# A batched row gather: three direct batches in place of five, smaller first index group, ranks summed by TensorE, first slot table in PSUM

## Chip, cores, metric

One core of a Trainium2 chip. The metric is the device time of one execution in microseconds. For one core a run is called slow when it lies over 1.5% above the fastest of the same kernel on the same chip.

## The reference

```python
x: [32, 512, 1024] float32;  indices: [32, 128] int
for b in range(32):
    result[b] = x[b, indices[b]]        # 128 rows of 4 KB
```

The indices are drawn once, the same for every run. Of a batch's 128 indices 109 to 120 are distinct.

## The kernel before

Five "direct" batches are gathered by an indirect DMA straight into their output block and stored. The other 27 read each distinct row once: VectorE and TensorE work out which indices are first occurrences (`lead`), give each a slot (`rank`, `slot`, `pack`), and turn that into row numbers per slot (`at`; a slot without a row gets a number out of bounds, which the gather skips). The gather fills one of eight buffers `u`. TensorE then multiplies `u` with a 0/1 matrix `s` ("spread", four matmuls of 128x512), ScalarE copies the result to the output block, and SyncE issues the store. Index work goes in groups of three batches, four groups ahead. For the first such batch (`HALF`) rows 0 to 255 are loaded whole and early (1.05 MB), and `half_rows` spreads those.

```python
HEAD, RING, GROUP, AHEAD, FAR = 5, 8, 3, 4, 1024
HALF = HEAD
...
for b in range(HEAD):
    gather(blocks[b], first[...] if b == 0 else idxT[:, b:b + 1], b)
    store(b)
...
def step0(g):      # compare all pairs of indices of each batch of the group
    bcs[g] = bc = pbc.tile([N, 4, N], F32, name="bc")
    for k, b in enumerate(of_group(g)):
        pe(mm, bc[:, k], lhsT=ident[:, b:b + 1].to_broadcast([N, N]), rhs=vf[:], start=True, stop=True)
    for k, b in enumerate(of_group(g)):
        dve(v.scalar_tensor_tensor, out=junk[:], in0=bc[:, k], scalar=idxF[:, b:b + 1], in1=below[:], ..., accum_out=cnt[:, b:b + 1])
    ...
    dve(v.tensor_scalar, out=cols(lead, g), in0=cols(cnt, g), scalar1=0.0, scalar2=None, op0=ALU.is_equal)
    for b in of_group(g):
        if b < B - 2:
            dve(v.tensor_tensor, out=past[:, b + 1:b + 2], in0=past[:, b:b + 1], in1=lead[:, b:b + 1], op=ALU.add)

def step1(g):      # ranks -> slots -> pack
    pe(mm, rk[:], lhsT=above[:], rhs=cols(lead, g), start=True, stop=False)
    pe(mm, rk[:], lhsT=every[:], rhs=cols(past, g), start=False, stop=True)
    ...
def step2(g):      # row numbers `at`, matrices `s`
    ...
step0(0)
step0(1)
for g in range(AHEAD):
    step1(g)
    if 0 < g < AHEAD - 1:
        step0(g + 1)
    step2(g)
    for b in of_group(g):
        if b < HEAD + RING:
            fetch(b)
    if g == 0:
        half_spread()
    elif g < 3:
        half_rows(g - 1, False)
for b in range(HEAD, B):
    spread_rows(b)
    fetch(b + RING)                      # waits until TensorE is done with this u
    g, step = divmod(b - HEAD, GROUP)
    if g + AHEAD < GROUPS:
        (step0, step1, step2)[step](g + AHEAD)
```

## Time and profile before

| | before |
|---|---|
| median of all runs (lowest to highest) | 87.55 us (87.08 to 88.76) |
| span of the profiled run | 85.6 us |
| DMA: bytes, mean rate | 32.91 MB, 384 GB/s |
| busy: TensorE, VectorE, ScalarE, GpSimd | 72, 37, 47, 39% |
| u gathers: issue to landing, median | 15.2 us |

A gather lands 15 us after its issue, because it stands in a long queue (the very first gather, with no other ahead of it, landed after 5.2 us). The DMA is the bound, and the queue is its stock. The lines that carry this are in the prediction.

How to read the profile lines: PE is TensorE, DVE is VectorE, ACT is ScalarE, POOL is GpSimd, SPq is the queue of SyncE. A timeline line gives start, duration, engine, source line, operation and tiles; in brackets stands how long the engine had been idle before, and what ended that. A line by stretch gives the busy time of each engine and ends with the granted TensorE clock, the busy share of the DMA engines and the rate in GB/s.

### The profile page before, as it was taken

How to read it: one execution, taken by the hardware profiler on the slowest of the kernel's cores; microseconds unless marked ns; L12 is line 12 of the kernel's file. 1: busy time of each engine (PE TensorE's matmuls, PEld its weight loads, DVE VectorE, ACT ScalarE, POOL GpSimd, SP SyncE). 2: the span in 40 equal slices, each digit the busy share in tenths (PEclk: the TensorE clock that was granted, in tenths of full speed). 3: DMA queues.
4: the chain of work that ended last, by engine and by line, in shares of the span. 5: the costliest groups of instructions: out<-in, count | busy, mean ns of one | idle time of the engine just before them, and what ended most of it. 6: DMA issues, size and time to landing. Idle time of an engine off the chain costs nothing.

```text
span 85.6 us, 827 instructions
## 1 busy us (share of the span) xinstructions
PE 61.3 (72%) x189; PEld 25.3 (29%) x189; DVE 31.6 (37%) x160; ACT 40.5 (47%) x63; POOL 33.3 (39%) x43
## 2 busy tenths in 40 slices
PE   0320379576999999999878987878789888889300
PEld 0300242323434444444333433322223333323000
DVE  4498793786563864844641453000000000000000
ACT  0899930000665665555554354455544554446400
POOL 6587578727444455554332444443320000000000
PEclk9999999999999999999999999999999999999996
DMA  0799999999999999999999999999999999999980
GB/s 1 274 375 344 302 342 415 415 417 417 419 419 419 417 421 419 415 419 417 419 419 419 417 419 413 421 413 423 417 417 419 419 419 419 423 415 417 423 337 15
DMA packets 9636, 32.91 MB, mean 384 GB/s; under 512 B 1584, under 2 KB 1616, under 8 KB 9632
## 3 DMA queue, kind: packets, MB, share of 16 engines
q1 hardware_dynamic: 4736, 16.81, 48.2%
q0 software_dynamic: 4608, 15.01, 44.7%
q10 hardware_dynamic: 288, 1.05, 3.3%
q8 instruction: 1, 0.02, 0.1%
q14 instruction: 3, 0.02, 0.1%
HBM read 17.86 MB, written 16.78 MB: 404 GB/s over the span
## 4 chain that ended last, share of the span: by engine, by line
DMA 40%; PE 21%; issue 14%; DVE 14%; POOL 3%; ACT 1%; SPq 0%; POOLq 0%; DVEq 0%
DMA u<-in_x_dram,at 37%; PE ps L24 20%; DVE junk L24 3%; POOL u L121 3%; DVE pack L24 3%; DMA vals<-in_indices_dram 2%; DVE past L24 2%; DVE nth L24 2%; DVE s L24 1%; PE pos L24 1%; DVE slot L24 1%; ACT block L250 1%; DVE lead L24 1%; DVE same L24 1%; SPq L68 0%
## 5 line engine op out<-in xcount | busy, mean ns | idle before, releaser
L24 PE MATMUL ps<-u,s 128*128 128x512 f32 x108 | 52.4, 611 | 6.8 <-DMA u<-in_x_dram,at 6.2
L121 POOL DMA_INDIRECT u<-in_x_dram,at x27 | 26.9, 997 | 26.7 <-PE ps L24 5.8
L250 ACT COPY block<-ps 128x512 f32<-128x512 f32 x36 | 21.1, 585 | 18.7 <-PE ps L24 17.6
L24 PEld LDWEIGHTS ps<-u,s 128*128 128x128 f32 x108 | 18.3, 189 | 29.1 <-ACT block L250 14.8
L250 ACT COPY pair<-ps 128x512 f32<-128x512 f32 x16 | 9.4, 585 | 8.7 <-PE ps L24 7.1
L24 DVE SCALAR_TENSOR_TENSOR junk<-bc,idxF,below 128x128 f16<-128x128 f32 x27 | 8.0, 347 | 7.1 <-PE bc L24 7.1
L24 ACT COPY u<-zero 128x1024 f32<-128x1024 f32 x8 | 7.7, 1040 | 0.0
L24 PE MATMUL pos<-near,pack 128*128 128x1 f16 x27 | 2.0, 167 | 5.6 <-DVE pack L24 5.6
L240 ACT COPY block<-ps 128x512 f32<-128x512 f32 x2 | 1.2, 585 | 10.1 <-PE ps L24 10.1
L24 PE MATMUL ps<-early,same 128*128 128x512 f32 x8 | 5.7, 854 | 0.0
L24 DVE TENSOR_TENSOR pack<-turn,slot 128x384 f16<-128x384 f16 (+2 forms) x10 | 5.1, 518 | 0.3
L24 DVE TENSOR_TENSOR s<-bc,at 128x384 f32<-128x384 f32 x9 | 5.0, 558 | 0.3
L24 PEld LDWEIGHTS <-pack 128*128 128x128 f16 x27 | 1.7, 99 | 9.5 <-DVE pack L24 7.4
L24 DVE TENSOR_TENSOR past<-past,lead 128x1 f16<-128x1 f16 x25 | 4.1, 163 | 0.9
L24 PE MATMUL bc<-vf,ident 128*128 128x128 f16 x27 | 3.4, 256 | 1.3 <-DVE same L24 1.3
L121 POOL DMA_INDIRECT block<-in_x_dram,idxT x4 | 3.8, 947 | 1.3 <-issue 0.9
L24 PEld LDWEIGHTS <-ident 128*128 128x128 f16 x27 | 2.4, 111 | 4.2 <-issue 4.2
L24 DVE TENSOR_SCALAR at<-pos 128x3 int32<-128x3 f32 x9 | 1.4, 160 | 5.1 <-PE pos L24 4.8
L24 DVE CAST nth<-rk 128x3 int32<-128x3 f32 x9 | 1.4, 160 | 3.7 <-PE rk L24 3.3
L21 PE MATMUL pos<-ident,vf 128*128 128x32 f16 x1 | 0.2, 210 | 3.6 <-DVE vf L24 3.6
L24 ACT ACT_TABLE_LOAD x1 | 1.3, 1283 | 2.5 <-DVE vf L24 2.5
L24 PEld LDWEIGHTS ps<-early,same 128*128 128x128 f32 x8 | 1.9, 257 | 1.5 <-issue 1.5
(32 smaller groups left out, 18.4 us busy)
## 6 DMA issues: line engine op xcount, KB each, us to landing
out_dram<-block SPq DMA_DIRECT2D x24, 512.0 KB, 8.0
out_dram<-pair SPq DMA_DIRECT2D x4, 1024.0 KB, 11.1
early<-in_x_dram ACTq DMA_DIRECT2D x2, 512.0 KB, 3.8
u<-in_x_dram,at POOLq DMA_INDIRECT x27, 15.2
block<-in_x_dram,idxT POOLq DMA_INDIRECT x4, 6.4
vals<-in_indices_dram SPq DMA_DIRECT2D x1, 32.0 KB, 2.0
first<-in_indices_dram SPq DMA_DIRECT2D x1, 1.0 KB, 1.8
block<-in_x_dram,first POOLq DMA_INDIRECT x1, 5.2
```

Of the source, the lines that this page charges most:

```text
L21: self.last = do(*args, **kw)
L24: self.last = do(*args, **kw)
L121: nc.gpsimd.indirect_dma_start(out=dst, out_offset=None, in_=xf[:], in_offset=bass.IndirectOffsetOnAxis(ap=at, axis=0), element_offset=b * ...
L240: nc.scalar.copy(out=blocks[HALF][:, w], in_=ps[:])
L250: nc.scalar.copy(out=blocks[b][:, w], in_=ps[:])
```

## The change

The intent: a direct batch reads all its 128 rows, repeated ones too, so fewer direct batches are fewer bytes. For that the row numbers of the first other batch must be ready sooner, so the first group has two batches, and its work is shortened. The sums over earlier batches of the group go to TensorE (more matmuls into `rk`) and `past` is advanced once per group later on. The table that `pack` compares with lies in PSUM for the first group; the last two batches, in place of the last one, use the second table, which is laid out anew. The order of steps changes with it, and so does the place of `half_rows`. Cut to its core:

```diff
-    HEAD, RING, GROUP, AHEAD, FAR = 5, 8, 3, 4, 1024
+    HEAD, RING, GROUP, AHEAD, FAR = 3, 8, 3, 4, 1024
+    APART = B - 2
+    groups = [range(HEAD, HEAD + 2), *(range(b, b + GROUP) for b in range(HEAD + 2, B, GROUP))]
...
-        pe(mm, rk[:], lhsT=above[:], rhs=cols(lead, g), start=True, stop=False)
-        pe(mm, rk[:], lhsT=every[:], rhs=cols(past, g), start=False, stop=True)
+        earlier = [(k, lead[:, groups[g][0]:groups[g][0] + like - k]) for k in range(1, like)]
+        if g:
+            earlier.append((0, past[:, g:g + 1].to_broadcast([N, like])))
+        pe(mm, rk[:, :n], lhsT=above[:], rhs=cols(lead, g), start=True, stop=not earlier)
+        for i, (k, more) in enumerate(earlier):
+            pe(mm, rk[:, k:like], lhsT=every[:], rhs=more, start=False, stop=i == len(earlier) - 1)
...
+        table = turn[:, 0:1] if g else bcs[0][:, GROUP:]
...
     step0(0)
-    step0(1)
     for g in range(AHEAD):
         step1(g)
-        if 0 < g < AHEAD - 1:
-            step0(g + 1)
-        step2(g)
-        for b in of_group(g):
+        if g == 1:
+            half_spread()
+        if g < AHEAD - 1:
+            spread_indices(g + 1)
+        fill_slots(g)
+        for b in groups[g]:
             if b < HEAD + RING:
                 fetch(b)
-        if g == 0:
-            half_spread()
-        elif g < 3:
-            half_rows(g - 1, False)
-    for b in range(HEAD, B):
-        spread_rows(b)
-        fetch(b + RING)
-        g, step = divmod(b - HEAD, GROUP)
-        if g + AHEAD < GROUPS:
-            (step0, step1, step2)[step](g + AHEAD)
+        if g > 1:
+            half_rows(g - 2, False)
+        if g < AHEAD - 1:
+            find_leads(g + 1)
+        match(g)
+    for g, batches in enumerate(groups):
+        steps = [(step0, g + AHEAD), (step1, g + AHEAD), (step2, g + AHEAD)]
+        for b in batches:
+            spread_rows(b)
+            fetch(b + RING)
+            for step, ahead in steps if b == batches[-1] else steps[:1]:
+                if ahead < len(groups):
+                    step(ahead)
+            steps = steps[1:]
```

(`spread_indices` and `find_leads` are the two halves of `step0`; `fill_slots` and `match` those of `step2`.)

## The prediction

> **What bounds the kernel now.** I read the page's slices first, then the DMA and rate columns by stretch, then the timelines of GpSimd, VectorE, TensorE and the store queue over the first 26 us.
>
> The slices, each 2.14 us:
>
> ```profile
> PE   0320379576999999999878987878789888889300
> DVE  4498793786563864844641453000000000000000
> DMA  0799999999999999999999999999999999999980
> ```
>
> The DMA row is full from the third slice to the end; no compute engine is. By stretch (last three columns: granted clock, DMA share, GB/s):
>
> ```profile
> 4.00:12.50 8.50, 2.64 (x20) 1.42 (x18) 7.58 (x46) 7.47 (x8) 5.80 (x6) 1.00 1.00 340
> 12.50:23.00 10.50, 8.20 (x31) 3.54 (x30) 6.69 (x32) 1.17 (x2) 6.63 (x7) 1.00 1.03 417
> 23.00:26.00 3.00, 3.00 (x13) 1.38 (x12) 1.92 (x11) 1.83 (x4) 1.33 (x2) 1.00 1.03 417
> 26.00:60.00 34.00, 30.16 (x94) 12.87 (x94) 13.79 (x65) 18.06 (x31) 15.71 (x16) 1.00 1.03 418
> ```
>
> From 12.5 us on the rate is flat at 417 to 419 GB/s. So the end is set by bytes left at 12.5 us over 0.418 MB/us: any byte saved is worth its time, and any hole in the DMA costs its whole length. What keeps it full is a stock of issued work, and its thinnest place is the hand-over from direct batches (gathered straight into their output block and stored) to those that go by a u buffer, TensorE and ScalarE. The timeline of GpSimd there:
>
> ```profile
> 8.06 0.95 POOL L121 DMA_INDIRECT block<-in_x_dram,idxT  x1 [0.30 <-issue]
> 9.96 1.01 POOL L121 DMA_INDIRECT u<-in_x_dram,at  x1 [0.96 <-ACT u L24]
> ...
> 20.27 1.00 POOL L121 DMA_INDIRECT u<-in_x_dram,at  x1 [0.30 <-issue]
> 22.34 1.00 POOL L121 DMA_INDIRECT u<-in_x_dram,at  x1 [1.07 <-PE bc L24]
> ```
>
> Eight u gathers are issued by 20.27; the ninth waits until TensorE has used a buffer up. TensorE and the store queue:
>
> ```profile
> 11.50 3.76 PE L24 MATMUL ps<-early,same 128*128 128x512 f32 x4
> ...
> 16.67 1.96 PE L24 MATMUL ps<-early,same 128*128 128x512 f32 x4
> ...
> 20.11 1.96 PE L24 MATMUL ps<-u,s 128*128 128x512 f32 x4
> ```
>
> ```profile
> 22.72 0.33 SPq L138 DMA_DIRECT2D out_dram<-block  x1
> ```
>
> The first u batch is spread at 20.11 and stored at 22.72. The packet records of the trace show that store's first packet at 26.2 and the ninth u gather's at 30.5; the five direct stores end at 23.8. In between the DMA lives on u gathers alone, and stays full (the row 23.00:26.00). All that is issued before the ninth u gather and that store is 9.8 MB; it would last until about 28. So the hand-over has 2 us to spare, and the change takes from that stock.
>
> **What the Trainium skill says.** "DMA: Bandwidth & Descriptors", section "Issuing engines are not separate DMA queues": transfers of all issuers share 16 engines. Here reads and writes together make 417 to 419 GB/s, and u gathers alone do so too (23 to 26 us): the trace agrees. "TensorE: Matmul & The Clock Gate", "Part 1: The HAM clock gate", says that a TensorE that was idle runs at half rate until about 3.4 us of sustained work. The same four matmuls took 3.76 us at 11.50 and 1.96 at 16.67 although the granted clock reads 1.00: agrees. "VectorE: DVE Perf Modes", "Why PSUM operands drop a tier", caps a float32 PSUM operand at 1x: 128x384 took 558 ns for s (PSUM) and 558 for pack (SBUF), so the table in PSUM costs nothing here. "SBUF — State Buffer", "SBUF: two separate sides", says that a VectorE operation with two SBUF inputs can block against a GpSimd operation that reads SBUF; the first pack (8.12, beside the gather of 8.06) took 0.56 like the rest, so I see no block for the PSUM table to lift.
>
> **The change, part by part.**
>
> *Bytes.* Batches 3 and 4 now leave repeated rows out. By the drawn indices 3664 rows were read and 3632 are: 32 x 4096 = 0.13 MB, at 0.418 MB/us 0.31 us. That is the whole gain in a full DMA.
>
> *Index work of the first group.* Before, rows appear (`at`) at 9.01 because both first groups' comparisons and 6 sums of `past` precede the ranks. After, with steps from the VectorE timeline: near 4.04, two junk (0.27 each) from 4.18, cnt 4.73, lead 4.92, two rk matmuls to 5.40, nth 5.47, mask 5.66, slot 5.87, pack (128x256, about 0.43) 6.07, two pos matmuls, `at` 6.74 to 6.90. From `at` to the gather took 0.79 before (9.17 to 9.96). So u gathers at 7.7 and 9.0, where direct ones stood at 6.81 and 8.06.
>
> *Second group.* Three junk from 6.93, lead 7.85, s (two batches) 8.06, past 8.42 and 8.62, rk, nth 9.06, pack 9.66, the two same 10.13 to 10.73. In TensorE's order the next bc matmuls (0.48, behind same) now stand ahead of pos: pos 11.3, `at` 11.55 to 11.71. Gathers 12.5, 13.8, 15.1.
>
> *Third group.* junk 11.74, lead 12.66, s 12.87, three past to 13.9, nth 14.18, pack 14.78, pos 15.39 to 15.63, `at` to 15.83. Gathers 16.6, 17.9, 19.2: all eight buffers taken, with batches 3 to 10 instead of 5 to 12.
>
> *Fourth group and first spread.* The two half_rows (the early rows' matmuls) stood after groups 2 and 3; now after 3 and 4. The first, cold, runs 15.6 to 19.2 (3.6) and rk of the fourth group stands behind it; from its end to the end of pos was 1.56 us before (15.26 to 16.82), so 20.8; the second 1.8, to 22.6. So the first spread starts at 22.6, not 20.1. Shifted by 2.5: its store is issued at 25.2 and the ninth gather at 24.8.
>
> *The stock.* By then issued: early 1.05 MB, three direct reads and stores 3.15, u gathers of batches 3 to 10 3.49 (852 rows): 7.7 MB. With before's rates to 12.5 and 417 beyond, it is gone at about 23. Next work: the gather's first packet comes 2.7 us after issue (2.77 to 5.48, 4.30 to 7.06 in the packet records): 27.5; the store's 1.4 (last store, idle queue) to 3.4 us (first) after: 26.6 to 28.6. Say 27.0: **a hole of 4 us where there was none.** Before had moved 0.47 (to 4.0) + 2.89 + 4.38 + 1.25 + 0.42 = 9.41 MB by 27.0. After: 7.68, with 0.13 less to move in all: (9.41 - 7.68 - 0.13) / 0.418 = 3.8 us later. Later on, TensorE delivers a batch per 1.9 us (GpSimd's spacing 22.34, 24.28), 0.98 MB, more than the 0.79 that the DMA moves in that time, so it fills again and stays full. Two more rk matmuls per group lie under this slack. Sum: 87.4 + 3.8 = 91.2; a warmer TensorE or quicker first packets can only make it less, so I say **91.0**.
>
> **The rivals.** (1) *The gain that is meant*: the DMA stays full, less bytes, and perhaps better feed while it runs at 340 (4 to 12.5 us). Time 86.5 to 87.1. For it: the first u gathers come earlier. Against: GpSimd gathers at about the same times as before up to 9 us and later after, and two batches of ready stores are gone. (2) *TensorE is warm for the first half_rows*: 1.8 us less, hole about 2 us, time 89.3. Against: the matmuls before it are as sparse as those ahead of 11.50. (3) *Holes between 10 and 23 us*, as u gathers come late one by one: these cost nothing more, because all of that stock is exhausted by 23 anyway; only a restart later than 27 does.
>
> **Range and chances.** The restart could lie between 25 and 28.3: 88.8 to 92.3. Within 2% (under 89.16) needs a first spread before 20.6, 2 us earlier than worked out: 0.16. Faster by 2% would need 1.7 us, five times what the bytes give: 0.03. Slower 0.81.
>
> **What would show it.** Right: DMA slices dip to near zero around 23 to 27 us, then full; `at` near 6.7, 11.6, 15.7, 21; the first spread near 22.6, the first u store near 25; one matmul group of early at about 3.7 us; the flat rate still 417 to 419; bytes read 17.73 MB. Wrong: no hole in that place, or the first spread before 21. If the hole is there but the time isn't longer, the stock after it was not the bound.

## The result and the profile after

| | before | after |
|---|---|---|
| median of all runs (lowest to highest) | 87.55 us (87.08 to 88.76) | 92.99 us (91.33 to 96.10) |
| ratio of the fast runs | | 1.0521, 95% interval 1.0454 to 1.0589 |
| bytes moved | 32.91 MB | 32.78 MB |

Ratios here and below compare fast runs with fast runs of the same rounds, so they are not quite the ratio of the medians. The change is slower.

The first profile after the change fell in the slow state. So I ran the unaltered kernel again (first experiment) and read its fast profile: 92.17 us, span 90.3. Its slices, the line of the DMA and that of its rate:

```profile
DMA  0898999999589999999999999999999999999960
GB/s 2 272 394 225 368 345 414 376 378 414 236 243 318 405 278 368 419 418 416 417 418 412 416 421 417 421 419 418 421 419 419 412 427 416 419 414 417 421 278 22
```

A slice is 2.26 us here. Where the kernel before shows nines without a break from the third slice on, the eleventh and twelfth slices are a 5 and an 8, and of the six from the eleventh on five move 236 to 368 GB/s. From the thirteenth on the busy share is back at 9 while the rate is not: a busy DMA row alone does not say that bytes move. By stretch, before:

```profile
23.00:29.00 6.00, 6.00 (x22) 2.73 (x21) 3.60 (x19) 3.63 (x7) 3.29 (x4) 1.00 1.03 419
29.00:38.00 9.00, 8.83 (x32) 3.94 (x31) 5.47 (x26) 5.73 (x10) 4.39 (x6) 1.00 1.03 418
```

and after, fast profile:

```profile
4.00:12.50 8.50, 2.19 (x21) 1.48 (x21) 6.54 (x38) 7.46 (x8) 3.93 (x5) 1.00 0.97 344
12.50:23.00 10.50, 7.39 (x28) 3.49 (x29) 6.27 (x32) 0.00 (x0) 5.96 (x6) 1.00 1.00 386
23.00:29.00 6.00, 4.74 (x20) 2.00 (x20) 3.24 (x16) 2.92 (x5) 1.99 (x2) 1.00 0.76 246
29.00:38.00 9.00, 9.00 (x37) 4.22 (x36) 5.24 (x27) 5.35 (x10) 4.87 (x5) 1.00 0.97 366
38.00:60.00 22.00, 22.00 (x79) 9.83 (x78) 10.65 (x52) 13.89 (x24) 11.34 (x13) 1.00 1.03 418
```

Up to 12.5 us the two are equal, and from 38 us on again. Nearly all the loss lies between (4.1 of 4.7 us, as is summed up below). Its cause stands in three timelines of the fast profile: GpSimd, TensorE, and the store queue.

```profile
17.68 1.00 POOL L126 DMA_INDIRECT u<-in_x_dram,at  x1 [0.31 <-DVE past L24]
18.98 1.00 POOL L126 DMA_INDIRECT u<-in_x_dram,at  x1 [0.30 <-issue]
24.11 1.00 POOL L126 DMA_INDIRECT u<-in_x_dram,at  x1 [4.13 <-PE bc L24]
26.05 1.00 POOL L126 DMA_INDIRECT u<-in_x_dram,at  x1 [0.94 <-PE rk L24]
29.45 1.00 POOL L126 DMA_INDIRECT u<-in_x_dram,at  x1 [2.40 <-PE bc L24]
```

```profile
15.20 3.52 PE L24 MATMUL ps<-early,same 128*128 128x512 f32 x4
...
20.16 1.96 PE L24 MATMUL ps<-early,same 128*128 128x512 f32 x4
21.95 1.88 PE L24 MATMUL ps<-u,s 128*128 128x512 f32 x4
23.84 1.94 PE L24 MATMUL ps<-u,s 128*128 128x512 f32 x4
25.61 0.17 PE L24 MATMUL rk<-lead,above 128*128 128x3 f16 x1
27.12 0.23 PE L24 MATMUL pos<-near,pack 128*128 128x1 f16 x3 [1.26 <-DVE pack L24]
```

```profile
24.48 0.33 SPq L143 DMA_DIRECT2D out_dram<-block  x1
```

After the eighth u gather (18.98) GpSimd waits 4.1 us for a free buffer (the view puts the end of the wait down to `bc`, the matmuls just behind the first spread), so nothing new enters the DMA between 18.98 and 24.11. The packet records of the trace show the last byte of the eighth gather at 24.7, the first packet of the first u store at 25.3 and that of the ninth gather at 27.0. So the DMA is quite empty for 0.6 us only; after that it is thin, with a single store and then a single gather to work on. Before, all of this overlapped with a stock that was still there.

**What a hole costs.** As the DMA runs at 418 GB/s from 38 us on (from 38 to 60 us it is 405 in e8 and 415 to 419 in all the others), the span should follow from what was moved by then: 38 us plus the rest over 0.418 MB/us, plus a tail for the last packets and the program's end. In all fourteen profiles it does, to within 1.6 us (rate from 0 to 38 us times 38; totals 32.91 MB with five direct batches, 32.82 with four, 32.78 with three by the indices):

| profile | MB by 38 us | 38 + rest / 0.418 | span | difference |
|---|---|---|---|---|
| before | 14.0 | 83.2 | 85.6 | 2.4 |
| after, fast (e1) | 12.2 | 87.3 | 90.3 | 3.0 |
| after, slow | 11.4 | 89.2 | 92.3 | 3.1 |
| e2 early half_rows | 12.8 | 85.8 | 88.2 | 2.4 |
| e3 warm | 12.1 | 87.4 | 90.8 | 3.4 |
| e4 five direct | 13.5 | 84.4 | 86.2 | 1.8 |
| e5 ten buffers | 12.9 | 85.6 | 87.9 | 2.3 |
| e6 before, ten buffers | 13.9 | 83.4 | 85.9 | 2.5 |
| e7 four direct | 12.0 | 87.9 | 90.8 | 2.9 |
| e8 four direct, repaired | 13.1 | 85.2 | 88.0 | 2.8 |
| e9 one step | 11.9 | 88.0 | 91.1 | 3.1 |
| e10 all three | 13.5 | 84.1 | 86.9 | 2.8 |
| e11 after, again | 12.6 | 86.2 | 88.6 | 2.4 |
| e12 one step, again | 12.7 | 86.0 | 88.5 | 2.5 |

The spans reach over 6.7 us, the differences from 1.8 to 3.4. So the first 38 us decide most of it. The table only adds up the loss; what causes it is for the experiments to show.

### The profile page after: what moved, and what is told of

The parts are those of the page before. It is cut to its first block, busy times and chain, and to the rows that moved or that the text cites. A ratio compares the mean times of both kernels' runs of the same rounds, so it can differ in the third digit from the quotient of the medians.

```text
span 92.3 us, 911 instructions
## 1 busy us (share of the span) xinstructions
PE 66.2 (72%) x220; PEld 28.1 (30%) x220; DVE 33.5 (36%) x170; ACT 42.9 (47%) x67; POOL 33.8 (37%) x46
## 2 busy tenths in 40 slices
DMA packets 9636, 32.78 MB, mean 355 GB/s; under 512 B 1616, under 2 KB 1648, under 8 KB 9632
## 3 DMA queue, kind: packets, MB, share of 16 engines
q10 hardware_dynamic: 288, 1.05, 3.2%
HBM read 17.86 MB, written 16.78 MB: 375 GB/s over the span
## 4 chain that ended last, share of the span: by engine, by line
DMA 34%; PE 33%; DVE 12%; issue 9%; POOL 2%; ACT 1%; SPq 0%; POOLq 0%; DVEq 0%
DMA u<-in_x_dram,at 32%; PE ps L24 29%; DVE junk L24 3%; DMA vals<-in_indices_dram 2%; POOL u L126 2%; DVE nth L24 2%; PE bc L24 1%; DVE s L24 1%; PE pos L24 1%; DVE pack L24 1%; DVE past L24 1%; DVE slot L24 1%; DVE lead L24 1%; PE rk L24 1%; ACT block L286 1%
## 5 line engine op out<-in xcount | busy, mean ns | idle before, releaser
L24 PE MATMUL ps<-u,s 128*128 128x512 f32 x116 | 55.4, 609 | 3.9 <-DMA u<-in_x_dram,at 3.2
L126 POOL DMA_INDIRECT u<-in_x_dram,at x29 | 29.0, 999 | 30.9 <-PE bc L24 12.1
L286 ACT COPY block<-ps 128x512 f32<-128x512 f32 x40 | 23.4, 586 | 20.1 <-PE ps L24 18.8
L24 PEld LDWEIGHTS ps<-u,s 128*128 128x128 f32 x116 | 20.2, 192 | 26.9 <-issue 14.1
L276 ACT COPY block<-ps 128x512 f32<-128x512 f32 x2 | 1.2, 586 | 13.9 <-PE ps L24 13.9
L24 PE MATMUL ps<-early,same 128*128 128x512 f32 x8 | 7.5, 1096 | 0.0
L24 DVE TENSOR_TENSOR s<-bc,at 128x384 f32<-128x384 f32 (+1 forms) x10 | 5.4, 541 | 0.2
L24 PE MATMUL rk<-lead,above 128*128 128x3 f16 (+1 forms) x10 | 1.8, 176 | 3.7 <-DVE lead L24 3.7
L24 DVE CAST nth<-rk 128x3 int32<-128x3 f32 (+1 forms) x10 | 1.6, 162 | 6.8 <-PE rk L24 5.0
L24 DVE TENSOR_SCALAR at<-pos 128x3 int32<-128x3 f32 (+1 forms) x10 | 1.6, 161 | 5.4 <-PE pos L24 5.0
L24 PEld LDWEIGHTS <-every 128*128 128x128 f16 x26 | 1.5, 102 | 3.9 <-issue 3.9
```

The lines of the kernel that those rows point to most:

```text
L24: self.last = do(*args, **kw)
L126: nc.gpsimd.indirect_dma_start(out=dst, out_offset=None, in_=xf[:], in_offset=bass.IndirectOffsetOnAxis(ap=at, axis=0), element_offset=b * ...
L276: nc.scalar.copy(out=blocks[HALF][:, w], in_=ps[:])
L286: nc.scalar.copy(out=blocks[b][:, w], in_=ps[:])
```

## The experiments

The calls ran on different chips (e1 to e4, e5 to e10 in two calls, e11 with e12), so ratios to the kernel before are compared across calls, and times only within one.

**e1: the changed kernel unaltered.** No edit.

> The changed kernel unaltered, for a profile in the fast state. Main theory (the hole at the hand-over is the loss, and its size follows the first spread): the fast profile shows the same hole, but the second pair of early matmuls at 1.96 us and not 3.76 as in the slow profile, so the first spread near 22.3 instead of 23.99 and the restart of the DMA near 26; time 91.5 to 92.3. Rival (the slow runs differ from the fast ones by DMA rate, not by TensorE): first spread at 24 in the fast profile too.

Measured: 92.92 us median (92.17 to 94.52, 4 runs), ratio 1.0559 (1.0448 to 1.067). The second pair of early matmuls took 1.96 us and the first spread began at 21.95, as the theory had it; the fast runs (92.17 to 93.32) came out at and above the top of the expected 91.5 to 92.3. The slow profile of the same kernel has, in its TensorE timeline,

```profile
20.44 3.76 PE L24 MATMUL ps<-early,same 128*128 128x512 f32 x4
23.99 1.97 PE L24 MATMUL ps<-u,s 128*128 128x512 f32 x4
```

so its first spread is 2.0 us later and its span 2.0 us longer. This fits the changed kernel's wide spread of times (90.5 to 96.1 us), if, with no stock, TensorE's rate in that moment goes straight into the time. The packed trace also holds the record of the granted TensorE clock: its first entry, full clock, is at 18.36 us in the fast profile and at 24.16 in the slow one. The slow profiles of e7 and e9 have both pairs at 3.76 too, while the five fast ones with three direct batches and the early matmuls in the late place (e1, e3, e5, e11, e12) have the second pair at 1.96. That TensorE's rate makes the slow state is not shown by this (e2's slow profile has its second pair at 1.96), and the loss itself is read from the fast profile alone.

**e4: five direct batches, all the rest of the change.**

```diff
-    HEAD, RING, GROUP, AHEAD, FAR = 3, 8, 3, 4, 1024
+    HEAD, RING, GROUP, AHEAD, FAR = 5, 8, 3, 4, 1024
-    groups = [range(HEAD, HEAD + 2), *(range(b, b + GROUP) for b in range(HEAD + 2, B, GROUP))]
+    groups = [range(HEAD, HEAD + 3), *(range(b, b + GROUP) for b in range(HEAD + 3, B, GROUP))]
```

> Five direct batches and a first group of three again; everything else of the change stays (ranks summed by TensorE, the first slot table in PSUM, two batches apart, the new order of steps). Main theory: the stock is back, no hole, time within 1% of the kernel before, 86.7 to 88.2 us. Rival (the added matmuls or the new order of steps cost by themselves): 89 us or more, with the DMA full at the hand-over or a hole there in spite of five direct batches.

Measured: 88.37 us median (87.87 to 88.53, 4 runs), ratio 1.0034 (0.9953 to 1.0116): the same as before. Its profile is the most telling of all. TensorE, GpSimd, and the DMA by stretch:

```profile
24.46 1.88 PE L24 MATMUL ps<-u,s 128*128 128x512 f32 x4
```

```profile
26.62 1.00 POOL L126 DMA_INDIRECT u<-in_x_dram,at  x1 [6.71 <-PE bc L24]
```

```profile
12.50:23.00 10.50, 6.55 (x23) 2.96 (x24) 7.07 (x37) 0.00 (x0) 5.89 (x6) 1.00 1.02 416
23.00:29.00 6.00, 6.00 (x20) 2.74 (x19) 1.57 (x10) 2.34 (x4) 1.44 (x2) 1.00 1.03 419
```

The first spread is *later* than in the changed kernel (24.46 against 21.95), the ninth gather too (26.62 against 24.11), and yet the DMA is full. So lateness alone is not the cause; lateness with a smaller stock is. The added matmuls, the new order and the PSUM table cost nothing that these runs can tell (the interval ends at 1.2%).

**e2: half_rows back to the place of the kernel before.**

```diff
-        if g > 1:
-            half_rows(g - 2, False)
+        if 0 < g < 3:
+            half_rows(g - 1, False)
```

> Only the two half_rows move back to where the kernel before has them, after the second and third group instead of the third and fourth. Main theory: the first pair runs about 11.5 to 15.2 us, the second about 17 to 19, first spread near 20.8, so the restart some 1.5 to 3 us earlier and the time 89 to 90.3 us, still over the kernel before since two direct batches of stock are missing. Rival (place of the early matmuls does not matter, the u gathers' late issue is what makes the hole): time as the changed kernel, 91.5 to 92.3.

Measured: 90.21 us median (89.8 to 91.77, 5 runs), ratio 1.0234 (1.0138 to 1.0331). This is over half of the loss back (1.0234 for 1.0559), and the fast runs (89.8 to 90.21) lie in the expected range; its profile, though slow, has the first spread at 20.45 and

```profile
23.00:29.00 6.00, 4.74 (x21) 2.18 (x20) 3.86 (x21) 2.50 (x6) 2.65 (x3) 1.00 0.98 354
```

where the changed kernel has 246. The place of the early rows' matmuls matters, once the stock is thin.

**e3: TensorE kept busy.** 25 matmuls without use (128x256, f16) in its waits up to 20 us.

```diff
+    def keep_busy(n):
+        if "busy" not in spread:
+            spread["busy"] = pout.tile([N, 512], F32, name="ps")
+        for _ in range(n):
+            pe(mm, spread["busy"][:, :2 * N], lhsT=every[:], rhs=turn[:].rearrange("p a b -> p (a b)"), start=True, stop=True)
     # called with 5, 7, 5, 3, 5 behind pos(0), rk(1), pos(1), bc(3), rk(3)
```

> 25 idle matmuls (128x256 f16) in TensorE's waits of the first 20 us, into a PSUM tile that the early rows' matmuls overwrite later; nothing else changed. Main theory: if they keep TensorE at full rate, the pairs of early matmuls take 1.96 us each, first spread near 21, time 89.8 to 90.8 and less spread between runs. If the pairs still take 3.76 us the time stays at 91.5 to 93. Rival (TensorE's rate has no part in it): pairs at 1.96 and the time unchanged.

Measured: 92.09 us median (91.28 to 92.58, 4 runs), ratio 1.0434 (1.0344 to 1.0524). The attempt did not do what it was made for:

```profile
7.36 1.23 PE L24 MATMUL ps<-turn,every 128*128 128x256 f16 x5
9.37 1.66 PE L24 MATMUL ps<-turn,every 128*128 128x256 f16 x7
11.67 1.23 PE L24 MATMUL ps<-turn,every 128*128 128x256 f16 x5
14.29 0.85 PE L24 MATMUL ps<-turn,every 128*128 128x256 f16 x3
15.51 3.50 PE L24 MATMUL ps<-early,same 128*128 128x512 f32 x4
```

The first pair still took 3.50 us (the clock record turns full at 18.63), so this run says nothing on what a warm first pair would be worth; the time stayed about where it was expected to stay in that case (91.5 to 93; it was 91.28 to 92.58).

**e5: ten u buffers.** **e6: the same on the kernel before.**

```diff
-    HEAD, RING, GROUP, AHEAD, FAR = 3, 8, 3, 4, 1024      # e6: 5, 8
+    HEAD, RING, GROUP, AHEAD, FAR = 3, 10, 3, 4, 1024     # e6: 5, 10
...
             spread_rows(b)
-            fetch(b + RING)
             for step, ahead in steps if b == batches[-1] else steps[:1]:
                 if ahead < len(groups):
                     step(ahead)
+            fetch(b + RING)
```

> The changed kernel with ten u buffers instead of eight (the fetch of a batch now stands behind the index step of the same turn, which its rows need). Main theory (the stock of issued work is what is short): gathers of batches 11 and 12 no longer wait for the first spread but only for the fourth group's rows, near 21 and 22.4 us instead of 24.1 and 26.1; 0.97 MB more stock, so up to 2.3 us back: 89.8 to 91 us. Rival (the hole comes from the first spread's lateness alone, whatever is gathered): 92 to 93, unchanged.

> The kernel before with ten u buffers (same move of the fetch): the control. Main theory: its DMA is already full at the hand-over, so two more buffers give nothing, 87.0 to 88.3 us, within 1% of the kernel before. Rival (more buffers help by themselves, for instance by deeper queues): more than 1% faster.

Measured: e5 91.05 us median (89.71, 90.34, 91.75, 92.29); two of its runs count as slow; the two fast ones have a mean of 90.0, beside 87.4 of the kernel before, which is 1.03 (the changed kernel's ratios were 1.0475 to 1.0559). e6 87.91 us median (87.35 to 88.52, 4 runs), ratio 1.0079 (0.9977 to 1.0182). In e5 (fast profile) the ninth and tenth gathers no longer wait for TensorE, and the hole is filled up to 369 GB/s (246 in e1) though the first spread (21.88) is as late as in e1:

```profile
21.18 0.99 POOL L126 DMA_INDIRECT u<-in_x_dram,at  x1 [1.49 <-issue]
22.48 1.00 POOL L126 DMA_INDIRECT u<-in_x_dram,at  x1 [0.30 <-issue]
```

```profile
23.00:29.00 6.00, 4.74 (x22) 2.05 (x21) 3.24 (x16) 2.86 (x5) 2.46 (x3) 1.00 1.01 369
```

More stock helps where stock is short (e5, by its profile and two fast runs) and shows no gain where it is not (e6). That was the theory's claim.

**e7: four direct batches, first group of one.** **e8: the same with half_rows early and ten buffers.**

```diff
-    HEAD, RING, GROUP, AHEAD, FAR = 3, 8, 3, 4, 1024
+    HEAD, RING, GROUP, AHEAD, FAR = 4, 8, 3, 4, 1024      # e8: 4, 10
-    groups = [range(HEAD, HEAD + 2), *(range(b, b + GROUP) for b in range(HEAD + 2, B, GROUP))]
+    groups = [range(HEAD, HEAD + 1), *(range(b, b + GROUP) for b in range(HEAD + 1, B, GROUP))]
     # e8 also has the edits of e2 and e5
```

> Four direct batches and a first group of one, else as the changed kernel. Main theory: one direct batch back is 1.05 MB of stock; batch 11 now waits for the fourth group's rows only: hole of 0 to 0.5 us and a thin time behind it, 88.3 to 90.3 us, between three direct batches and five. Rival (the loss is tied to something that only three direct batches meet): 87.5 like five.

> Four direct batches, first group of one, early rows' matmuls at the place of the kernel before, ten u buffers: all that the theory says restores the stock while one more batch drops its repeated rows. Main theory: no hole, 87.0 to 88.3 us, even with the kernel before or some 0.1 to 0.2 us under it, which these rounds cannot tell. Rival (GpSimd's 1.3 us per gather is the bound once direct stores end): 88.5 to 90.

Measured: e7 91.09 us median (90.62 to 93.49, 5 runs), ratio 1.0407 (1.0316 to 1.0499). e8 89.5 us median (88.55 to 90.37, 4 runs), ratio 1.0179 (1.0077 to 1.0281). Both are worse than I expected: e7's fast runs (90.62 to 91.09) lie above the 88.3 to 90.3 of the theory, and those of e8 (88.55 to 89.8) in the range of its rival, GpSimd's pace. The hole at 23 us is smaller than in e1, but a second one follows. e7's TensorE and its DMA (slow profile):

```profile
26.60 0.18 PE L24 MATMUL rk<-lead,above 128*128 128x3 f16 x1 [1.21 <-DVE lead L24]
28.12 0.23 PE L24 MATMUL pos<-near,pack 128*128 128x1 f16 x3 [1.26 <-DVE pack L24]
28.21 1.96 PE L24 MATMUL ps<-u,s 128*128 128x512 f32 x4
```

```profile
29.00:38.00 9.00, 9.00 (x37) 4.08 (x36) 4.89 (x28) 5.41 (x10) 3.99 (x4) 1.00 0.81 282
```

The loop puts all the steps that a group has left behind its last batch. With a group of one all three steps of the fifth index group follow the first spread; TensorE waits twice for VectorE inside them, the next spread begins at 28.21 and the next gather at 30.44. I had left this out. In e8 the hole at 23 us is gone and the second one is there (fast profile):

```profile
23.00:29.00 6.00, 3.43 (x15) 1.36 (x12) 3.35 (x16) 1.17 (x2) 3.14 (x4) 0.78 1.03 410
29.00:38.00 9.00, 9.00 (x36) 4.13 (x35) 4.72 (x26) 5.25 (x9) 4.31 (x5) 0.96 1.01 364
```

As the DMA stays at 410 to 29 us, GpSimd's pace is not what e8 loses by. The clock column shows something that I had not looked for: by the clock record TensorE had half its clock from 26.31 to 29.72, after those waits, and the second spread took 3.56 us in place of 1.96. So this pair does not grade the stock cleanly, and the ratio of e8 lies between those of e2 and of the kernel before, no more.

**e9 and e12: one index step per batch, as before.** **e11: the changed kernel beside e12.** In the fast profile of e1 the same wait is there in smaller form (25.61 to 27.12, quoted above).

```diff
-    for g, batches in enumerate(groups):
-        steps = ...                                # see the change
+    todo = [(step, g) for g in range(AHEAD, len(groups)) for step in (step0, step1, step2)]
+    for b in range(HEAD, B):
+        spread_rows(b)
+        fetch(b + RING)
+        if todo:
+            step, g = todo.pop(0)
+            step(g)
```

> The changed kernel with one index step per batch in the main loop, as the kernel before has it, in place of two steps behind the last batch of the first group of two; nothing else changed. The traces of the changed kernel show TensorE standing 1.3 us between rk and pos of the fifth group (25.61 to 27.12) and the DMA at 362 to 371 GB/s from 29 to 38 us. Theory (this wait is what keeps the DMA thin after the hole): no such wait, 29 to 38 us at 400 or more, about 1 us back, 90.7 to 91.6 us. Rival (it is thin because the gathers come at GpSimd's pace or the hole just lasts): unchanged, 91.9 to 92.6.

> The changed kernel once more, beside e12 on the same chip and in the same rounds, as the effect of one index step per batch (about 1 us) is lost between calls: 91.5 to 92.5 us in the fast runs, ratio 1.045 to 1.056.

> One index step per batch again. Theory (TensorE's wait behind the first group keeps the DMA thin from 29 to 38 us): fast runs 0.7 to 1.3 us under those of e11. Rival (no effect of its own): within 0.4 us of e11.

Measured: e9 92.32 us median (90.6 to 94.1, 4 runs, two of them fast: 90.6 and 91.73), ratio 1.0435 (1.0314 to 1.0556); e11 92.05 us median (90.49 to 94.58, 6 runs), ratio 1.0475 (1.0384 to 1.0565), and e12 92.14 (90.29 to 94.20, 6 runs), ratio 1.047 (1.0375 to 1.0566). The fast runs of e11 (90.49 to 91.48) lie below the 91.5 to 92.5 that I expected, so e9's times alone say nothing; beside e11 the expected 0.7 to 1.3 us did not come with e12. Fast profiles of e11,

```profile
23.00:29.00 6.00, 4.74 (x24) 2.31 (x21) 3.69 (x19) 2.93 (x5) 2.37 (x3) 1.00 0.86 298
29.00:38.00 9.00, 9.00 (x38) 3.99 (x37) 4.92 (x25) 5.32 (x10) 4.60 (x5) 1.00 1.01 372
```

and of e12:

```profile
23.00:29.00 6.00, 6.00 (x27) 2.75 (x25) 3.24 (x16) 3.54 (x7) 3.00 (x3) 1.00 0.78 259
29.00:38.00 9.00, 9.00 (x37) 4.06 (x35) 5.37 (x27) 5.55 (x10) 5.00 (x5) 1.00 1.02 407
```

The wait is gone from TensorE (6.00 us busy of 6.00 against 4.74), and the stretch behind the hole is fuller by 35 GB/s x 9 us = 0.32 MB, 0.75 us. But this execution's hole is deeper by 39 x 6 = 0.23 MB, 0.56 us; its first index work had started 0.36 us later (pos of the first group at 6.54 against 6.18). So the mechanism is there and its worth in time is not shown. Up to 1 us could hide in intervals of 0.9% to either side; the point estimate is nil.

**e10: all three repairs on three direct batches** (e2, one step per batch, nine buffers; the fetch behind the step).

> Three direct batches with all three repairs: early rows' matmuls at the place of the kernel before, one index step per batch, nine u buffers. Theory (the parts of the loss add up: late first spread, thin time behind it, too little stock): 87.9 to 89.2 us, near the kernel before but not under it, as between the last direct store and the first spread only gathers run and GpSimd issues one (0.46 MB) per 1.3 us, 0.35 MB/us against the 0.418 that the DMA can move. Rival (the repairs are not additive, all act on the same hole): 89.5 to 90.3, like the early matmuls' place alone.

Measured: 89.5 us median (88.86 to 90.87, 4 runs), ratio 1.0245 (1.0157 to 1.0333): by ratio no better than e2 alone (1.0234, on another chip). The mean of its fast runs, 89.3, falls between the two expected ranges; the theory's sum of the parts (87.9 to 89.2) did not come. Its fast profile:

```profile
12.50:23.00 10.50, 7.87 (x36) 3.39 (x35) 6.77 (x34) 1.76 (x3) 7.17 (x8) 1.00 0.99 380
23.00:29.00 6.00, 6.00 (x28) 2.85 (x27) 3.25 (x17) 3.61 (x7) 3.00 (x3) 1.00 1.00 380
29.00:38.00 9.00, 9.00 (x33) 3.96 (x33) 5.40 (x25) 5.63 (x10) 4.98 (x5) 1.00 1.03 417
```

The time behind 29 us is mended, the hole is gone, and what is left is a rate of 380 between 12.5 and 29 us, worth (417 - 380) x 10.5 + (419 - 380) x 6 = 0.62 MB, 1.5 us. The packet records show the direct stores ended at 17.6 and the first u store begun at 24.3: between them only gathers run, which GpSimd issues at one per 1.3 us at best. That this pace holds the rate there is argued, not shown apart, and it can't be all: the trace has 359 GB/s from 12.5 to 17.6, with direct stores still running, 386 from 17.6 to 24.3 and 392 from 24.3 to 29, so about half of the 0.62 MB, 58 x 5.1 = 0.30, is lost before the stores end. What held the rate there stays open (GpSimd had stood idle for 2.0 us before its gather of 11.67, which may be it). No version with fewer than five direct batches beat the kernel before, so the experiments point to none.

## Why the prediction was right

It said 91.0 us (88.8 to 92.3) and slower. The ratio is 1.0521, and the fast runs beside it lie from 91.33 to 92.21, in the upper half of the range (4.6 us over the fast runs before, where 3.6 were said); the median over all runs, slow ones too, is 92.99 and above it. By its steps, beside the fast profile (e1):

- **The flat rate and the bytes.** 418 GB/s from 38 us on, 32.78 MB. Right.
- **The index chain.** `at` said for 6.7, 11.6, 15.7 and 21; the VectorE timeline has 7.23, 11.54, 15.38 and 20.33. The eight u gathers were said for 7.7 to 19.2; they were issued from 8.18 to 18.98. Right to 0.7 us, worked out from the durations of the profile before alone.
- **The PSUM table gives nothing.** `pack` of 128x256 took 0.42 us from PSUM in the slow profile, and 426 ns from SBUF in the kernel before (a two-batch pack of its last group). Right.
- **TensorE cold for the first pair and in the way of the fourth group's ranks.** 3.52 us from 15.20, the second pair 1.96, first spread at 21.95 where 22.6 was said. Right, and e2 shows that the place costs some 2.7 us of time (means of the fast runs 92.7 and 90.0). One reading beside it was wrong: the prediction set the slow pair against a granted clock of 1.00. The clock record of the kernel before begins at 16.09 us, with full clock; the 1.00 that the views print before that is the lack of a record. So the record agrees with a TensorE that turns fast between the two pairs.
- **Two batches less of stock.** Shown by e4 (stock back, hole gone, though the spread is later), e5 (more buffers, hole gone) and e6 (no gain on the kernel before).
- **The size: right as a sum, from two terms that were off and cancel.** I had the DMA run dry at 23, restart at 27.0 and run full from there. In fact the 7.7 MB of stock, sized right (7.73 MB moved by then), lasted to 24.7, as the DMA ran at 386 and not 417 GB/s from 12.5 us on; the first u store's packets came 0.83 us after its issue, at 25.3; the restart was earlier, but the DMA then stayed thin until 38 us. So the empty time was 0.6 us and not 4. In bytes: by 29 us the kernel before had moved 353 x 29 = 10.24 MB and the changed one 305 x 29 = 8.85; less the 0.13 saved, that is 3.0 us. From 29 to 38 us another (418 - 366) x 9 = 0.47 MB, 1.1 us. Together 4.1, for 3.8 said; the spans differ by 4.7, and the rest lies behind 38 us. That the two errors nearly cancel is luck. The step that failed is "it fills again and stays full": I took TensorE's 1.9 us per batch from a stretch of the kernel before in which one index step goes with each batch, and did not see that the changed loop puts two steps behind the second batch. What that step is worth stays open: e12 took the wait away and filled the stretch (407 GB/s), but its time did not fall.
- **The rivals.** The DMA was not full (1). The holes from 10 to 23 us (3) are there, 386 GB/s in place of 417. In e1 they add nothing, as I said: all that had been issued was moved by 24.7, before the next packet at 25.3. A warm first pair (2) was not seen in any profile of the changed kernel, and e3 failed to make one.
- **Small misreadings.** The direct stores of the kernel before end at 23.96 by the packet records, not 23.8, so the row 23:26 is not of gathers alone at its start; from 24.0 to 26.2 the rate is 419, and the reading stands. The sign "bytes read 17.73 MB" could not come, as that line of the page reads 17.86 in both kernels (see the last section).

## What to carry to other kernels

When one resource is full from end to end, ask how long its stock of issued work lasts at the thinnest place, in bytes over rate, before you trade some of that work for fewer bytes: here 0.13 MB saved (0.31 us) was paid with 2 MB of stock at the one place where the next work comes late. Off-path engines need not be faster for this, only early enough, so work out when each stream of work can start again and compare it with when the stock runs out. And a total moved by a fixed moment (here by 38 us, behind which all run at nearly one rate) tells from a single profile, to within some 1.6 us here, what that execution lost, even where the times scatter.

## What the Trainium skill lacked or had wrong

- "DMA: Bandwidth & Descriptors", "Specifications", gives a first-byte latency of about 1 us for transfers issued by GpSimd and 0.6 us for those by the sync and scalar engines. Here the first packet of an indirect gather of 128 rows came 2.7 to 2.9 us after its issue began, also with no other gather queued (24.11 to 26.97 in e1, beside one store). A store's came 0.83 us after issue with the queues empty and 3.4 us after with gathers ahead (7.97 to 11.39 before). The page has no separate figure for the indirect form.
- "TensorE: Matmul & The Clock Gate", "Part 1: The HAM clock gate", doesn't say what share of busy time counts as sustained work. In e3 TensorE was busy for 5.51 of 8.5 us (4 to 12.5 us) in bursts of up to 1.7 us, and the next matmuls still ran at the slow rate (3.50 us for four).
- In no page did I find the time from a VectorE result to the indirect gather that waits for it: 0.79 us here (`at` ends at 9.17, gather at 9.96), against 0.30 us between gathers that wait for nothing. Nor that the profile's HBM read line counts skipped rows: it reads 17.86 MB in both kernels, though the DMA bytes fell by 0.13 MB; 17.86 is what 32 x 128 rows of 4096 bytes, the early rows and the indices come to (16.78 + 1.05 + 0.03).
